# The order of the engines' queues, worked out by another of the tile layer's planners

## The chip, the cores and the metric

The kernel runs on one core of a Trainium2 chip. The metric is the device time of one execution in microseconds. Five engines work side by side, each through a queue of its own, strictly in order: TensorE (PE, matmuls and transposes), VectorE (DVE), ScalarE (ACT), GpSimd (POOL) and SyncE (SP, which issues the weight loads). An instruction whose operand isn't there yet holds up everything behind it on its engine.

## What is computed

Two transformer blocks, one after the other, on 256 rows of 1024 features, in fp32. Cut to what matters:

```python
def first_block(x, mem, ...):                       # 4 layers
    for i in range(4):
        kind = i % 3     # 0: top-k index attention, 1: dilated attention, 2: block attention
        mix = attention[kind](x @ w_in[...])        # rotary on q, k; layer norm on the index keys
        mo  = memory_attention(qm, mem_n @ w_mem_kv[i])
        x = layer_norm(ALPHA * x + concat(mix, mo) @ w_out[i])
        g, u = split(x @ w_gate_up[i])              # swiglu, 2816 wide
        x = layer_norm(ALPHA * x + (silu(g) * u) @ w_down[i])

def second_block(x, p, ...):                        # 2 layers
    for l in range(2):
        u = rms_norm(x) @ w_in[l]                   # differential, latent and sliding-window attention
        y = sum(gate_b * ((o_b * silu(z_b)) @ w_br_b[l]) for b in (a, b, c))
        x = x + rms_norm(y @ w_out[l])              # "post-norm"
        x = x + sigmoid(x @ w_ple_gate[l]) * (p[l] @ w_ple_proj[l])
```

## The kernel before

The 256 rows are two streams of 128 rows, t = 0 and 1. Each stream is a Python generator that goes through all six layers; the loop at the end of the program (L1193 to L1206) advances them in turn, stream 1 four weight units behind stream 0, so that each weight is loaded once and used by both.

A weight unit is 256 rows of at most 512 columns (`ensure`, L316): a DMA on SP's queue into `raw` (three buffers), a cast to the high part `H` on ScalarE (L330) and the rest `L` = raw - H on VectorE (L331), seven buffers of each. Activations are split likewise into `xH` and `xL`. A product is then three matmuls for each 128 rows: H with xH (L375), L with xH (L376), H with xL (L377), the output in an `mm` bank of 128 rows by up to 512 columns.

Whatever a stream has to do besides matmuls of weights is written at the place where it is wanted, or put off by some units (`defer`, `job`, `tick`, L340 to L362). The steps that matter here:

- Transposes of activations on TensorE (L398) into a `w` bank, copied out as a split: cast L413 on ScalarE and difference L414 on VectorE (L409 and L410 with a scale, L391 and L393 without a split).
- The swiglu: tanh L893 on ScalarE, L894 and the product with the up half L896 on VectorE, then `h_T` (L885) transposes the result `nat` by L398.
- Layer norms of the first block: L451, L452, then L459 and L461 on VectorE, then transposes of `x`.
- Rotary steps on GpSimd (L217 to L220), index keys on VectorE (L792 to L796) with their transposes L802.
- Dilated attention: scores L472, L727 on VectorE, exponential L731 on ScalarE, transposes L498, product L509, normalisation L516 on VectorE.
- The post-norm of the second block: square L1155 on ScalarE and copy L1157 on VectorE of each half, sum L1160, power on GpSimd (L425, L427), scale L1165 and add L1167 on VectorE for each half, transposes L398 of `x`.

The program text does not fix the order of the queues. The tile layer takes the instructions with their dependences, puts them into one queue for each engine by a list scheduler that keeps a clock of its own, and adds the semaphore waits.

Of the kernel before, what the change touches and what calls it, by code (L numbers as in the profile page):

```python
# [65 lines left out]
def tile_two_blocks(  # L66
# [7 lines left out]
    nc = tc.nc  # L74
# [24 lines left out]
    def bcast_row(ap2d, n):  # L99
        return bass.AP(tensor=ap2d.tensor, offset=ap2d.offset, ap=[[0, P], [1, n]])  # L100

# [1 line left out]
    xt = [xp.tile([P, D], F32, tag=f"x{t}", name=f"x{t}") for t in range(2)]  # L103
    cst = cp.tile([P, C_DIL], F32, name="cst")
    posi = cp.tile([P, 2, 2], I32, name="posi")
# [113 lines left out]
        eng.tensor_tensor(out=t2[:, :, half:], in0=v[:, :, :half], in1=bc(s[:, half:]), op=ALU.mult)  # L219
        eng.tensor_tensor(out=v, in0=t1, in1=t2, op=ALU.add)  # L220

# [1 line left out]
    units = []  # L223

    seq = [0]
# [156 lines left out]
        yield from gemm_part(t, acc, ck.units, xh, xl, True, True)  # L382
        return acc

# [1 line left out]
    evac_n = [0]  # L386

    def evac(dst, src, scale=None):
# [127 lines left out]
        vec.tensor_tensor(out=dst, in0=o.rearrange("p (h w) -> p h w", w=w),  # L516
                          in1=r[:, :n].unsqueeze(2).to_broadcast([P, n, w]), op=ALU.mult)

# [1 line left out]
    memT = [xp.tile([P, 4, 2 * P], F32R, tag=f"m{k}", name=f"memT{k}") for k in range(4)]  # L520

    mem_rows = []
# [50 lines left out]
            tick(t)  # L573
        evac(mem_kv[layer][:, which], acc)

# [1 line left out]
    bias_rep = dp.tile([12, P, 384], F32, tag="bias_rep", name="bias_rep")  # L577

    def prepare_bias():
# [75 lines left out]

        return job(t, a, b, c)

# [1 line left out]
    def block1(t):  # L659
        nkt = t + 1  # L660
        nk = nkt * P
# [244 lines left out]
                add_norm(t, half, acc, st)  # L906
            xT = finish_norm(t, st, gt, bt, i + 1 < DEPTH)

# [1 line left out]
    def block2(t):  # L910
        nkt = t + 1
        nk = nkt * P
# [343 lines left out]
```

## Time and profile before

| | us |
|---|---|
| median of 3 runs | 1982.85 (1980.98 to 1984.48) |
| the profiled execution, its own time | 1982.1 |
| span of the profiled execution | 1982.1 |
| TensorE busy in it | 1940.6 |
| VectorE, ScalarE, GpSimd busy | 1240.0, 981.2, 211.0 |

A row of the page or of a view names the engine, the line of the program, the operation and its tiles (out<-in, with the numbers of buffers left out). Idle time in front of an instruction is in square brackets, with the engine and line whose result ended it. A matmul's listed duration reaches from its start to its modelled end; since matmuls overlap, the pace is read from one start to the next.

### The profile page before, as it was taken

To read this page: it belongs to the slowest core of one execution; us is meant where nothing else is said; L and a number is where in the kernel's file an instruction comes from. 1 tells how busy PE (TensorE), PEld (TensorE's weight loads), DVE (VectorE), ACT (ScalarE), POOL (GpSimd) and SP (SyncE) were. 2 spreads that over 40 slices of the span, in tenths; PEclk is the share of its full clock that TensorE was granted. 3 is DMA by queue.
4 is the path that set the end of the run, shared out by engine and by line. 5 is a ranking of instruction groups with operands and counts; after the bars stand their busy time and mean duration, and the time that the engine had idled before them with its cause. 6 is when DMAs were issued, how large, how long until landed. Compare 5 with 4: busy or idle time off the path is not lost. (4 is left out here: it accounts for less than half of the span.)

```text
span 1982.1 us, 27405 instructions
## 1 busy us (share of the span) xinstructions
PE 1940.6 (98%) x10013; PEld 1612.5 (81%) x10013; DVE 1240.0 (63%) x2148; ACT 981.2 (50%) x1650; POOL 211.0 (11%) x358
## 2 busy tenths in 40 slices
PE   7999999999999999999999999999999999999998
PEld 6888778888888878888877878887888887888886
DVE  5857555657665565765567576556666667566565
ACT  5654444444444455444445544445654456665453
POOL 4020000011000012000020200002121111111010
PEclk9999999999999999999999999999999999999999
DMA  6635666544665653565654356566446655445653
GB/s 197 187 99 158 209 184 199 182 136 131 209 182 174 198 169 107 158 192 155 211 178 134 105 161 191 159 208 175 119 145 179 186 177 168 120 141 149 188 184 106
DMA packets 198295, 327.55 MB, mean 165 GB/s; under 512 B 12914, under 2 KB 70838, under 8 KB 198160
## 3 DMA queue, kind: packets, MB, share of 16 engines
q1 hardware_dynamic: 191072, 306.03, 51.1%
q0 software_dynamic: 5312, 17.44, 2.8%
q10 hardware_dynamic: 1776, 2.33, 0.3%
q8 instruction: 79, 1.29, 0.3%
q14 instruction: 56, 0.46, 0.1%
HBM read 324.68 MB, written 3.43 MB: 166 GB/s over the span
## 5 line engine op out<-in xcount | busy, mean ns | idle before, releaser
L331 DVE TENSOR_TENSOR L<-raw,H 128x1024 fp32r<-128x1024 f32 (+3 forms) x616 | 727.7, 1182 | 452.3 <-ACT H L330 447.5
L330 ACT CAST H<-raw 128x1024 fp32r<-128x1024 f32 (+3 forms) x616 | 615.5, 1000 | 593.6 <-PE mm L377 457.8
L375 PE MATMUL mm<-H,xH 128*128 128x512 f32 (+3 forms) x1904 | 741.9, 391 | 1.9 <-ACT H L330 1.7
L377 PE MATMUL mm<-H,xL 128*128 128x512 f32 (+3 forms) x1904 | 717.7, 378 | 2.1 <-DVE xL L406 1.7
L376 PE MATMUL mm<-L,xH 128*128 128x512 f32 (+3 forms) x1904 | 716.0, 377 | 0.0
L375 PEld LDWEIGHTS mm<-H,xH 128*128 128x128 f32 x1904 | 358.6, 188 | 73.3 <-issue 5.0
L377 PEld LDWEIGHTS mm<-H,xL 128*128 128x128 f32 x1904 | 358.2, 188 | 71.3 <-DVE xL L406 3.1
L376 PEld LDWEIGHTS mm<-L,xH 128*128 128x128 f32 x1904 | 359.4, 189 | 55.9 <-DVE L L331 0.5
L375 PE MATMUL mm<-H,hH 128*128 128x512 f32 x352 | 137.6, 391 | 0.0
L376 PE MATMUL mm<-L,hH 128*128 128x512 f32 x352 | 137.2, 390 | 0.0
L377 PE MATMUL mm<-H,hL 128*128 128x512 f32 x352 | 137.0, 389 | 0.0
L423 POOL TENSOR_SCALAR pw_in<-mv 128x1 f32<-128x1 f32 x22 | 15.1, 690 | 822.1 <-DVE mv L432 822.0
L489 ACT ACTIVATE sm<-sm,mn 128x128 f32<-128x128 f32 (+1 forms) x136 | 60.9, 449 | 42.2 <-DVE mn L485 41.9
L398 PE MATMUL w<-cst,nat 128*128 128x128 f32 (+1 forms) x436 | 69.9, 276 | 11.3 <-DVE nat L896 6.2
L377 PEld LDWEIGHTS mm<-H,hL 128*128 128x128 f32 x352 | 66.1, 188 | 13.7
L375 PEld LDWEIGHTS mm<-H,hH 128*128 128x128 f32 x352 | 66.1, 188 | 13.1
L376 PEld LDWEIGHTS mm<-L,hH 128*128 128x128 f32 x352 | 66.1, 188 | 13.1
L398 PEld LDWEIGHTS w<-cst,nat 128*128 128x128 f32 (+1 forms) x436 | 51.8, 139 | 29.4 <-DVE nat L896 9.6
L413 ACT CAST xH<-w 128x512 fp32r<-128x512 f32 (+1 forms) x64 | 33.4, 532 | 53.9 <-PE w L398 51.9
L217 POOL TENSOR_TENSOR rope<-nat,rc 128x128 f32<-128x128 f32 (+1 forms) x38 | 20.2, 532 | 326.8 <-ACT nat L624 286.5
L498 PE MATMUL w<-cst,sm 128*128 128x128 f32 x304 | 52.5, 276 | 0.4
L398 PE MATMUL w<-cst,x 128*128 128x128 f32 x192 | 31.3, 290 | 15.4 <-DVE x L461 5.3
(262 smaller groups left out, 2023.4 us busy)
## 6 DMA issues: line engine op xcount, KB each, us to landing
raw<-in_w_gate_up_dram SPq DMA_DIRECT2D x160, 512.0 KB, 3.7
raw<-in_w_in_dram SPq DMA_DIRECT2D x104, 512.0 KB, 3.6
raw<-in_w_down_dram SPq DMA_DIRECT2D x88, 512.0 KB, 4.4
raw<-in_w_out_dram SPq DMA_DIRECT2D x48, 512.0 KB, 3.5
raw<-in_w_in_a_dram SPq DMA_DIRECT2D x56, 256.0 KB, 3.0
raw<-in_w_in_a_dram SPq DMA_DIRECT2D x16, 512.0 KB, 5.1
raw<-in_w_mem_kv_dram SPq DMA_DIRECT2D x16, 512.0 KB, 4.1
raw<-in_w_gate_up_dram SPq DMA_DIRECT2D x32, 256.0 KB, 2.8
```

Source lines behind the costliest of these rows:

```text
L217: eng.tensor_tensor(out=t1, in0=v, in1=bc(c), op=ALU.mult)
L330: act.copy(h, raw)
L331: vec.tensor_tensor(out=lo, in0=raw, in1=h.bitcast(F32), op=ALU.subtract)
L375: pe.matmul(a, xh[:, kt, :], h[:, j, :], start=st, stop=False)
L376: pe.matmul(a, xh[:, kt, :], lo[:, j, :], start=False, stop=False)
L377: pe.matmul(a, xl[:, kt, :], h[:, j, :], start=False, stop=en)
L398: pe.transpose(tr[:width, j, :], src(j), ident)
L413: act.copy(h, tr[:, :n, :])
L423: pool.tensor_scalar(v[:, :n], src, eps, None, op0=ALU.add)
L489: act.activation(sm[:, j, :], src, AF.Exp, bias=mn[:, j : j + 1], scale=-1.0, accum_out=sums[:, j : j + 1])
L498: pe.transpose(tr[:, j * nkt + kt, :], sm[:, j, kt * P : (kt + 1) * P], ident)
```

## The change

One argument is added where the tile layer is opened; the scheduler then keeps its clock with its timeline simulator. The other lines of the diff only drop comments. Instructions, buffers and data stay; SP's queue keeps its order word for word.

```diff
-    with tile.TileContext(nc) as tc:
+    with tile.TileContext(nc, schedule_with_timeline_sim=True) as tc:
         tile_two_blocks(tc, *args)
```

Three places show what moves. In the rows, numbers behind a name tell buffers apart.

TensorE, swiglu of layer 0 of the first block; `mm_2507` is a product of stream 0, `mm_2475` one of stream 1, `nat_2395` the swiglu's result of stream 0 that the transposes L398 read. The order before:

```order
L375 MATMUL mm_2507<-H_2510,xH0_1777 128x512
L376 MATMUL mm_2507<-L_2511,xH0_1777 128x512
L377 MATMUL mm_2507<-H_2510,xL0_1778 128x512
L398 MATMUL w_2526<-cst_83,nat_2395 128x128 x4
L375 MATMUL mm_2475<-H_2426,xH1_1952 128x512
```

And now:

```order
L375 MATMUL mm_2475<-H_2426,xH1_1952 128x512
L376 MATMUL mm_2475<-L_2427,xH1_1952 128x512
L377 MATMUL mm_2475<-H_2426,xL1_1953 128x512
L375 MATMUL mm_2475<-H_2444,xH1_1952 128x512
L376 MATMUL mm_2475<-L_2445,xH1_1952 128x512
L377 MATMUL mm_2475<-H_2444,xL1_1953 128x512
L375 MATMUL mm_2507<-H_2535,xH0_1777 128x512
L375 MATMUL mm_2475<-H_2444,xH1_1952 128x512
L398 MATMUL w_2526<-cst_83,nat_2395 128x128 x4
```

The transposes have moved behind eleven matmuls: a unit and a half of stream 1 and the first matmul of stream 0's next unit, which before came after them.

TensorE, end of the dilated layer; `sm_4372` is the last head's exponentials of stream 0, `PT_4434` their transposes, `b2_0_3467` the attention's output of stream 0, `xH0_4270` its split. The order before:

```order
L498 MATMUL w_4432<-cst_83,sm_4372 128x128
L377 MATMUL mm_4419<-H_4320,xL1_4408 128x512
L472 MATMUL w_4486<-b1_0_3466,b1_1_3565 128x128
L509 MATMUL w_4436<-b1_0_3466,PT_4434 128x192
L398 MATMUL w_4441<-cst_83,b2_0_3467 128x128 x2
L472 MATMUL w_4486<-b1_1_3565 128x128
```

And now:

```order
L498 MATMUL w_4432<-cst_83,sm_4372 128x128
L509 MATMUL w_4436<-b1_0_3466,PT_4434 128x192
L398 MATMUL w_4441<-cst_83,b2_0_3467 128x128 x4
L375 MATMUL mm_4282<-H_4450,xH0_4270 128x512
L376 MATMUL mm_4282<-L_4451,xH0_4270 128x512
```

Four steps that feed each other by way of other engines (L498, L509, L398, L375) now stand in direct succession; the scores L472 and the matmul of stream 1 that stood between them come earlier.

VectorE, post-norm of the first of the second block's two layers; `x0_81` is the stream's `x`, `nat_14476` and `nat_14556` are its two halves, `nat_14652` is of stream 1. The order before:

```order
L1157 COPY nat_14556<-mm_14478 128x512
L1160 TENSOR_TENSOR tot_14558<-ssq_14371 128x1
L331 TENSOR_TENSOR L_14642<-raw_14639,H_14641 128x1024
L1165 SCALAR_TENSOR_TENSOR nat_14476<-nat_14476,pw_out_14562,gg_14369 128x512
L1165 SCALAR_TENSOR_TENSOR nat_14556<-nat_14556,pw_out_14562,gg_14369 128x512
L1167 TENSOR_TENSOR x0_81<-x0_81,nat_14476 128x512
L1167 TENSOR_TENSOR x0_81<-x0_81,nat_14556 128x512
L331 TENSOR_TENSOR L_14695<-raw_14692,H_14694 128x1024
```

And now:

```order
L1157 COPY nat_14556<-mm_14478 128x512
L1160 TENSOR_TENSOR tot_14558<-ssq_14371 128x1
L331 TENSOR_TENSOR L_14695<-raw_14692,H_14694 128x1024
L331 TENSOR_TENSOR L_14713<-raw_14710,H_14712 128x1024
L1165 SCALAR_TENSOR_TENSOR nat_14476<-nat_14476,pw_out_14562,gg_14369 128x512
L1165 SCALAR_TENSOR_TENSOR nat_14556<-nat_14556,pw_out_14562,gg_14369 128x512
L1157 COPY nat_14652<-mm_14548 128x512
L1160 TENSOR_TENSOR tot_14654<-ssq_14467 128x1
L1167 TENSOR_TENSOR x0_81<-x0_81,nat_14476 128x512
L331 TENSOR_TENSOR L_14731<-raw_14728,H_14730 128x1024
L1167 TENSOR_TENSOR x0_81<-x0_81,nat_14556 128x512
```

Two splits and the other stream's copy and sum have moved ahead of the adds L1167, and a third split stands between them. On TensorE the transposes of `x` stand 15 matmuls behind the last matmul of the product that L1157 copies, before 24.

## Rows read from the trace of the kernel before

**Rows 1.** The page, part 1: busy time, share of the span, instructions.

```profile
PE 1940.6 (98%) x10013; PEld 1612.5 (81%) x10013; DVE 1240.0 (63%) x2148; ACT 981.2 (50%) x1650; POOL 211.0 (11%) x358
```

**Rows 2.** Timeline of TensorE and VectorE at a swiglu: start, duration, instruction, [idle].

```profile
240.77 0.66 PE L398 MATMUL w<-cst,nat 128*128 128x128 f32 x4 [1.83 <-DVE nat L896]
...
241.50 0.39 PE L376 MATMUL mm<-L,xH 128*128 128x512 f32 x1
241.73 0.40 PE L377 MATMUL mm<-H,xL 128*128 128x512 f32 x1
...
238.65 1.22 DVE L331 TENSOR_TENSOR L<-raw,H 128x1024 fp32r<-128x1024 f32 x1
...
240.04 0.68 DVE L896 TENSOR_TENSOR nat<-nat,mm 128x512 f32<-128x512 f32 x1
```

**Rows 3.** Waits of TensorE: line, what for, us in total, times, longest.

```profile
PE w L398 <- DVE nat L896: 6.2, 6, 1.8
PE w L398 <- DVE x L461: 5.3, 9, 1.5
PE w L398 <- DMA cst<-in_const_dram: 4.0, 1, 4.0
PE w L398 <- POOL nat L220: 3.7, 9, 0.7
PE w L398 <- DMA x<-in_x_dram: 3.5, 1, 3.5
PE w L802 <- DVE ki L796: 2.8, 3, 1.3
PE w L398 <- DVE x L1167: 2.4, 4, 0.8
PE mm L377 <- DVE xL L406: 1.7, 2, 0.9
PE mm L375 <- ACT H L330: 1.7, 1, 1.7
PE mm L377 <- DVE pT L414: 1.4, 2, 0.7
PE w L802 <- DVE mv L432: 0.8, 1, 0.8
```

**Rows 4.** The page, part 5: groups by line; busy, mean ns, idle before, releaser.

```profile
L330 ACT CAST H<-raw 128x1024 fp32r<-128x1024 f32 (+3 forms) x616 | 615.5, 1000 | 593.6 <-PE mm L377 457.8
```

**Rows 5.** Timeline of TensorE, shortly after the first loads.

```profile
12.41 0.63 PE L377 MATMUL mm<-H,xL 128*128 128x512 f32 x1
12.84 0.63 PE L375 MATMUL mm<-H,xH 128*128 128x512 f32 x1
```

**Rows 6.** Timeline of VectorE and TensorE at the first post-norm.

```profile
1634.28 0.68 DVE L1157 COPY nat<-mm 128x512 f32<-128x512 f32 x1
...
1636.92 1.42 DVE L1165 SCALAR_TENSOR_TENSOR nat<-nat,pw_out,gg 128x512 f32<-128x512 f32 x2 [0.47 <-POOL pw_out L427]
1638.25 1.29 DVE L1167 TENSOR_TENSOR x<-x,nat 128x512 f32<-128x512 f32 x2
...
1637.80 0.39 PE L377 MATMUL mm<-H,xL 128*128 128x512 f32 x1
1639.00 1.26 PE L398 MATMUL w<-cst,x 128*128 128x128 f32 x8 [0.81 <-DVE x L1167]
```

**Rows 7.** Timeline of TensorE and ScalarE at the end of the dilated layer.

```profile
471.45 0.27 PE L498 MATMUL w<-cst,sm 128*128 128x128 f32 x1
...
474.90 0.72 PE L375 MATMUL mm<-H,xH 128*128 128x512 f32 x2
...
477.00 0.94 ACT L731 ACTIVATE sm<-sm,mn 128x768 f32<-128x768 f32 x1 [2.27 <-DVE mn L727]
```

**Rows 8.** Timeline of ScalarE, start of the feed-forward part, layer 0.

```profile
173.55 1.05 ACT L330 CAST H<-raw 128x1024 fp32r<-128x1024 f32 x1 [1.41 <-issue]
174.50 0.59 ACT L391 ACTIVATE mkv<-mm 128x512 f32<-128x512 f32 x1
```

## The prediction

> **What bounds the kernel now.** I read the page first: TensorE is busy 1940.6 us, 98% of a span of 1982.1, VectorE 63%, ScalarE 50% [rows 1]. A busy matmul is not a matmul at its peak, so the next view is TensorE's own rows: 512-column matmuls start 0.227 us apart all through the kernel, although each is listed at 0.39 us (the starts 241.50 and 241.73 in [rows 2]). At that pace the engine is full. What an order of the queues can give or take is therefore only TensorE's idle time: 1982.1 - 1940.6 = 41.5 us. The view of TensorE's waits says where it lies [rows 3]: 4.0 + 3.5 us are the first loads, which no order of these instructions shortens; after the last matmul some 5 us pass; about 27 us are short waits between 30 and 1960 us. The longest of these is 1.83 us. A wait of w us costs about w + 0.16, because a matmul that finds TensorE empty loses the overlap of 0.39 - 0.227.
>
> Who is late in these waits is nearly always VectorE (L896, L461, L1167, L796): a short step there stands behind weight splits L331 of 1.22 us, or the ScalarE step ahead of it behind casts L330 of 1.05 us. The 616 casts fill 616 us [rows 4], and as many splits somewhat more; TensorE needs their results in turn, but not each of them soon.
>
> **What the change does to the queues.** Every instruction stays, and the weight loads on SP's queue keep their order, so matmul time and bytes stay, and I cost them at nothing. What moves is the order on TensorE, VectorE and ScalarE: by some 16 places each on TensorE and VectorE. So the sum is a list of waits that go and waits that come, place by place.
>
> **Waits that go.** I take the TensorE work that stands between the matmul that starts a chain and the transposes or matmuls that need its end, in the old and in the new order, at 0.227 us a matmul.
> (a) Swiglu, L398 after L896. Before, 12 matmuls (2.7 us) stand between the end of the up product and the transposes; VectorE starts L896 at 240.04, because a split started at 238.65 is ahead of it, and TensorE stands still 1.83 us [rows 2]. After, 23 matmuls (5.2 us) stand there, against at most 4.5 us from matmul to the end of L896 in the six cases. All six waits go: 6.2 us.
> (b) Norm of the first block (L461): distance 4.9 to 6.2 us becomes 9.4 to 9.6 at five of nine waits; 2.6 of the 5.3 us go; the rest has the same distance or gets worse (below).
> (c) Rotary step on GpSimd (L220): seven of nine waits, 3.25 of 3.7 us. (d) Index keys (L796 and L432): distances 3.7 to 8.2 become 8.4 to 12.2; 2.8 + 0.8 us. (e) Entry of the second block and the branches (L406, L414 and four small ones): distance 2.7 becomes 7.5; 4.4 us. (f) The one wait for a cast, near the start: nine more matmuls (2.0 us) stand ahead of it; 1.65 us.
> Sum [rows 3]: 6.2 + 2.6 + 3.25 + 3.6 + 4.4 + 1.65 = 21.7 us in 32 waits; with 32 x 0.16 it is 26.8 us.
>
> **Waits that come.** The trace cannot show these; each is built from durations and bounded by the same chain in the old order.
> (g) Post-norm of the second block, twice (1639 and 1952 us). The chain is copy L1157, the power L427 on GpSimd, scale L1165, add L1167, transposes [rows 6]. Before, the last matmul ahead starts at 1637.80, so the transposes could start at 1638.03 and start at 1639.00: 0.97 late. After, nine matmuls fewer stand ahead: 0.97 + 9 x 0.227 = 3.0 late with the old VectorE order. That order is worse too: two splits instead of one stand ahead of L1165, the second waiting for a cast whose buffer comes free only 1.4 us of TensorE work ahead of the transposes; then L1165 twice (1.33 from start to start), L1157 with the small L1160 (0.7), L1167 (0.65, half of the two): with the cast's 1.05 that is 1.05 + 1.22 - 1.4 + 2.7 = 3.6 late, some 3.8 with the hand-overs. Third, a split now stands between the two adds: the second four transposes wait 1.22 + 0.65 - 0.4 = 1.5 more at the first place, and 0.6 at the second, where four matmuls stand between. 5.3 and 4.4 take the place, at each, of 0.97 and a wait of 0.4 on the other stream: 9.7 - 2.7 = +7.0 us. Ends: twice 3.0 - 0.97 = +4, and +9.
> (h) End of the dilated layer, stream 0 (about 474 us): four steps that feed each other now stand back to back on TensorE (L498, L509, L398, L375). Before, 471.45 to 474.90 pass between the first and the last of them without a wait [rows 7]; of that time the new order fills only 0.9 us, so some 2.5 us are lost; with a split and two L727 ahead of L516, and the exponential L731 (0.94) ahead of L413, 3.8. Two smaller ones of the kind at 444 and 465 us: 1.3. Together 5.1; ends 2.5 and 7.
> (i) Start of the feed-forward part in layers 0 and 2: on ScalarE a third cast and the copy L391 are put ahead of both L413, which stood ahead of them [rows 8]: 1.05 + 0.59 = 1.6 each, 3.2.
> (j) Attention of the two index layers at 776 and 1111 to 1120 us: 2.5. (k) Norms at 1157 and 1358 us: 1.4 + 2.7. (l) Three small ones: 1.4.
> Sum: 7.0 + 5.1 + 3.2 + 2.5 + 4.1 + 1.4 = 23.3 us. All of these come from places where steps that feed each other were pushed together; none is measured, so the range takes them at half and at more.
>
> The net is 23.3 - 26.8 = -3.5 us against the profiled execution's 1982.1: 1978.6; the median of the runs is 0.75 above that execution, so about **1979 us**.
>
> A count speaks for a small gain. Of 1,112 results that TensorE takes from the other engines, I set the work ahead of the reader against the shortest chain: less than 2 us to spare have 268 before and 144 after; nothing to spare have 16 before and 34 after. The order widens the middle and sharpens the tail.
>
> **Rivals.** A run of this kernel can tell 0.2%, about 4 us, from no change.
> 1. *The new waits are small, 1968 us.* Each lets VectorE and ScalarE catch up, so the next place is early, and a wait that comes twice in my list is paid once. With (g) to (l) at half, 12: 1982.85 - 26.8 + 12 = 1968. For it: 268 to 144, and casts idle 458 us for want of free buffers [rows 4], so these engines have time. Against it: the back-to-back rows of (g) and (h) can't be shortened by a rested engine below 4 + 2.5 us.
> 2. *Slower: the split ahead of the result that TensorE stands waiting for, 1990 us.* In (g) the new order puts splits, some for weights needed far later, ahead of a result that nothing covers. If that holds at half of the 18 results that are newly without room, 9 x 1.22 = 11 us are added: 1990; at all of them, less the five that the sum has already, 1995. It decides for slower from some six of them on (6 x 1.22 = 7.3 over 1979 is 4 over the old time). For it: the cause of the old waits is just this, in [rows 2]. Against it: VectorE is idle 37% of the span, and a split often waits for its cast while the short step runs.
> [...]
> 4. *The order does not change.* Excluded: on TensorE 7,501 rows of the two listings differ.
>
> **How the numbers follow.** Forecast as summed, 1974 to 1984: 0.40, of which 0.18 lies under 1978.9 (faster by over 0.2%) and 0.22 within. Rival 1: 0.26, faster. Rival 2: 0.20, slower. Rival 3: 0.10, slower. Nothing that can be measured for other reasons: 0.04. So faster 0.18 + 0.26 = 0.44, same 0.22 + 0.04 = 0.26, slower 0.20 + 0.10 = 0.30. Cases of both signs hold much of this; the forecast's own range is 1974 to 1984. The range goes from rival 1 with a little more, 1967, to rival 2 with a little more, 1992; it leaves out some 0.06 below and 0.09 above.
>
> **What would show it.** In TensorE's waits after: no rows for L896 and L796, at most 0.5 us for L220, under 3 us for L461 apart from 1157 and 1358; a new entry for L1167 of 8 to 10 us in four to six waits, with one of over 3 us; waits for L516, L413 and L391 near 474 us. Matmul time within 3 us of 1940.6 by the pace, else my costing of the moved matmuls at nothing is wrong. If the swiglu waits stay, the distance in the order is not what sets them, and (a) to (f) fall. If L1167 shows under 2.4 us, (g) falls and rival 1 is right. [...]

## The result: slower by 1.7%, a third of it idle time on TensorE and two thirds longer matmuls

| | before | after |
|---|---|---|
| median, us | 1982.49 | 2017.64 (2015.37 to 2021.11, four runs) |
| ratio, 95% interval | | 1.0172 [1.0157, 1.0188] |
| span of the profiled execution | 1982.1 | 2015.7 |
| TensorE busy | 1940.6 | 1963.1 |
| TensorE idle | 41.5 | 52.6 |
| mean granted clock of TensorE | 1.000 | 0.983 |

The forecast was 1979, with 1992 as the upper end. The change cost 35 us. In the profiled executions the 33.6 us are 11.1 us more idle time and 22.5 us more busy time on TensorE, for the same instructions. First the page of the kernel after, parts 1 and 2 (busy time, and the granted clock in 40 slices), which answer to [rows 1]:

```profile
PE 1963.1 (97%) x10013; PEld 1638.9 (81%) x10013; DVE 1237.0 (61%) x2148; ACT 977.6 (48%) x1650; POOL 212.9 (11%) x358
...
PEclk9979999999999999999999999999999999999999
```

The third slice (101 to 151 us) has a 7. Before, every slice has a 9. Next TensorE's waits of the kernel after (engine and line that waits, the one waited for, us in total, times, the longest), which answer to [rows 3]:

```profile
PE w L398 <- DVE x L461: 11.2, 5, 3.7
PE w L398 <- DVE x L1167: 11.0, 3, 5.3
PE mm L375 <- ACT H L330: 5.1, 2, 4.1
PE mm L375 <- ACT xH L413: 5.0, 7, 1.5
...
PE w L398 <- DVE b L516: 2.3, 3, 1.5
...
PE w L398 <- POOL nat L220: 0.5, 1, 0.5
```

The swiglu's L896 and the index keys' L796 have no row any more, and the rotary step L220 kept 0.5 us: these waits went as forecast. Two groups grew. L1167 was forecast. L461 was not: 11.2 us in five waits against 5.3 us in nine.

**Where L461 is late.** Three of the five are at the ends of layers 0 to 2, at 385, 714 and 1044 us: 3.69, 3.50 and 2.58 us. VectorE at the first of them, in the kernel before (start, us, engine, line, operation, count, idle time ahead):

```profile
373.40 0.68 DVE L451 SCALAR_TENSOR_TENSOR x<-x,mm 128x512 f32<-128x512 f32 x1
...
374.99 1.23 DVE L331 TENSOR_TENSOR L<-raw,H 128x1024 fp32r<-128x1024 f32 x1
376.13 1.41 DVE L459 SCALAR_TENSOR_TENSOR x<-x,mv,gg 128x512 f32<-128x512 f32 x2
377.45 1.41 DVE L461 SCALAR_TENSOR_TENSOR x<-x,pw_out,gb 128x512 f32<-128x512 f32 x2
```

And after, with TensorE's row that waits:

```profile
377.21 0.68 DVE L451 SCALAR_TENSOR_TENSOR x<-x,mm 128x512 f32<-128x512 f32 x1
...
378.79 1.22 DVE L331 TENSOR_TENSOR L<-raw,H 128x1024 fp32r<-128x1024 f32 x1 [0.17 <-ACT H L330]
...
380.15 1.23 DVE L331 TENSOR_TENSOR L<-raw,H 128x1024 fp32r<-128x1024 f32 x1
381.29 1.41 DVE L459 SCALAR_TENSOR_TENSOR x<-x,mv,gg 128x512 f32<-128x512 f32 x2
382.80 1.23 DVE L331 TENSOR_TENSOR L<-raw,H 128x1024 fp32r<-128x1024 f32 x1
383.95 0.68 DVE L451 SCALAR_TENSOR_TENSOR x<-x,mm 128x512 f32<-128x512 f32 x1
384.55 1.41 DVE L461 SCALAR_TENSOR_TENSOR x<-x,pw_out,gb 128x512 f32<-128x512 f32 x2
...
385.44 1.94 PE L398 MATMUL w<-cst,x 128*128 128x128 f32 x8 [3.69 <-DVE x L461]
387.20 0.79 PE L375 MATMUL mm<-H,xH 128*128 128x512 f32 x1
387.79 0.63 PE L376 MATMUL mm<-L,xH 128*128 128x512 f32 x1
388.22 0.48 PE L375 MATMUL mm<-H,xH 128*128 128x512 f32 x1
388.54 0.40 PE L376 MATMUL mm<-L,xH 128*128 128x512 f32 x1
```

From L451 to L461 pass 4.05 us before and 7.34 us after: two more splits, and the other stream's L451. TensorE's last matmul ahead starts 4.15 us behind L451 in both (377.55 and 381.36), so the difference turns into a wait. Behind it the matmuls start 0.59 and 0.43 us apart, and only from 388.5 on 0.23.

**The clock.** The granted clock in windows around that wait and around the first post-norm (window, its length, busy time and count of each engine, the granted clock of TensorE, DMA share, GB/s), kernel after:

```profile
384.80:388.20 3.40, 2.76 (x10) 2.40 (x11) 3.40 (x6) 1.78 (x3) 0.00 (x0) 0.53 0.49 150
388.20:392.00 3.80, 3.80 (x18) 3.12 (x17) 3.31 (x7) 0.00 (x0) 2.30 (x3) 0.97 0.36 102
...
1668.00:1675.00 7.00, 4.36 (x13) 3.12 (x14) 6.27 (x12) 1.62 (x3) 3.48 (x3) 0.53 0.52 165
```

The clock's records in the two profiled executions hold two values, 1.00 and 0.50. At 0.50, called half rate here, 512-column matmuls behind the first post-norm start 0.43 us apart (1673.09, 1673.52, 1673.95); ahead of it, at 1.00, 0.23 us (1664.07, 1664.30, 1664.52). The kernel after is at 0.50 in nine stretches between its first matmuls and its last few microseconds: from 122.2 us for 23.9 us; for 3.4 us each at 385.0, 716.1, 1043.8 and 1187.1; and for 6.8 us each at 490.8, 801.4, 1668.4 and 1982.4. Together that is 65 us at half rate, so at most 32 us lost, and less where TensorE idled in them; 22.5 us were measured as busy time. The kernel before has no such stretch in its profiled execution; its other executions record mean clocks from 1.000 (in one of 1978.56 us) down to 0.997 (in one of 1986.76 us), so some of them have a few.

Eight of the nine lie at or just behind waits, of 0.7 us to 5.3 us. The longest stretch doesn't. Windows over it, restricted to L375, the first matmul of each weight product (window, length, busy time and count on TensorE and of its weight loads, granted clock, DMA share, GB/s), before:

```profile
120.00:125.00 5.00, 0.95 (x2) 0.38 (x2) 1.00 0.26 96
125.00:130.00 5.00, 1.50 (x4) 0.75 (x4) 1.00 0.30 105
130.00:135.00 5.00, 1.45 (x4) 0.68 (x4) 1.00 0.06 8
135.00:140.00 5.00, 1.28 (x3) 0.44 (x3) 1.00 0.41 120
```

and after:

```profile
120.00:125.00 5.00, 0.00 (x0) 0.00 (x0) 0.72 0.63 211
125.00:130.00 5.00, 0.00 (x0) 0.00 (x0) 0.50 0.00 0
130.00:135.00 5.00, 0.00 (x0) 0.00 (x0) 0.50 0.00 0
135.00:140.00 5.00, 0.00 (x0) 0.00 (x0) 0.50 0.00 0
```

The new planner put all weight matmuls out of this stretch, so that from 117.05 to 144.91 us TensorE's queue holds nothing but the attention's small matmuls (L472, L498, L509, L398, 64 to 256 columns each). TensorE counts as busy all that time (by ends that are modelled), and its only wait there of over 0.1 us is 0.55 us, 0.4 us ahead of the fall. Before, two to four weight products stand in every 5 us among the same small matmuls.

### The profile page after: what moved, and what is told of

The parts are those of the page before. It is cut to its first block, busy times and chain, and to the rows that moved or that the text cites. A ratio compares the mean times of both kernels' runs of the same rounds, so it can differ in the third digit from the quotient of the medians.

```text
span 2015.7 us, 27443 instructions
## 1 busy us (share of the span) xinstructions
PE 1963.1 (97%) x10013; PEld 1638.9 (81%) x10013; DVE 1237.0 (61%) x2148; ACT 977.6 (48%) x1650; POOL 212.9 (11%) x358
## 4 chain that ended last, share of the span: by engine, by line
PE 92%; DVE 3%; DMA 2%; ACT 2%; issue 1%; POOL 1%; ACTq 0%; DVEq 0%; POOLq 0%
PE mm L375 25%; PE mm L377 25%; PE mm L376 25%; PE w L472 5%; PE w L398 4%; PE w L509 3%; PE mm L571 2%; PE w L498 2%; DVE L L331 1%; ACT H L330 1%; DMA raw<-in_w_gate_up_dram 1%; DMA raw<-in_w_ple_gate_dram 0%; DMA posi<-in_positions_dram 0%; DVE x L459 0%; DMA raw<-in_w_in_b_dram 0%
## 5 line engine op out<-in xcount | busy, mean ns | idle before, releaser
L375 PE MATMUL mm<-H,xH 128*128 128x512 f32 (+3 forms) x1904 | 728.7, 385 | 10.5 <-ACT H L330 5.1
L376 PE MATMUL mm<-L,xH 128*128 128x512 f32 (+4 forms) x1904 | 725.8, 382 | 1.3 <-DVE L L331 1.2
L375 PEld LDWEIGHTS mm<-H,xH 128*128 128x128 f32 x1904 | 361.1, 190 | 79.3 <-ACT xH L413 8.8
L375 PE MATMUL mm<-H,hH 128*128 128x512 f32 x352 | 137.2, 390 | 0.0
L375 PEld LDWEIGHTS mm<-H,hH 128*128 128x128 f32 x352 | 66.2, 188 | 13.3
L413 ACT CAST xH<-w 128x512 fp32r<-128x512 f32 (+1 forms) x64 | 32.5, 532 | 86.7 <-PE w L398 86.6
L398 PE MATMUL w<-cst,nat 128*128 128x128 f32 (+1 forms) x436 | 69.3, 275 | 0.5 <-POOL nat L220 0.5
L398 PEld LDWEIGHTS w<-cst,nat 128*128 128x128 f32 (+1 forms) x436 | 54.1, 142 | 11.2 <-POOL nat L220 0.8
L498 PE MATMUL w<-cst,sm 128*128 128x128 f32 x304 | 60.5, 290 | 0.6 <-DVE mn L485 0.5
L414 DVE TENSOR_TENSOR xL<-w,xH 128x512 fp32r<-128x512 f32 (+1 forms) x64 | 38.3, 618 | 36.8 <-ACT xH L413 36.4
L398 PE MATMUL w<-cst,x 128*128 128x128 f32 x192 | 33.5, 318 | 27.0 <-DVE x L461 11.2
```

Source lines behind the costliest of these rows:

```text
L375: pe.matmul(a, xh[:, kt, :], h[:, j, :], start=st, stop=False)
L376: pe.matmul(a, xh[:, kt, :], lo[:, j, :], start=False, stop=False)
L398: pe.transpose(tr[:width, j, :], src(j), ident)
L414: vec.tensor_tensor(out=lo, in0=tr[:, :n, :], in1=h.bitcast(F32), op=ALU.subtract)
L498: pe.transpose(tr[:, j * nkt + kt, :], sm[:, j, kt * P : (kt + 1) * P], ident)
```

## The experiments

**Theory W** (waits): the new waits at the norms, post-norms and the dilated layer make the kernel slower, with the clock's fall behind each as a part of its price. **Theory C** (clock): at 122 us it is the kind of work that stands together on TensorE, with no wait at all, and that alone costs some 10 us. **Rival**: the loss is spread over the whole order and belongs to no place.

All kernels are the kernel before with the same addition, a table that fixes each engine's queue, as an order of issue and without waits. Only the table differs, unless said otherwise: with VectorE alone edited, for instance, TensorE's and ScalarE's rows stand in the trace in the very order of the kernel that was edited.

```diff
         tile_two_blocks(tc, *args)
+        pin(tc, nc)
+
+def pin(tc, nc):
...
+            if prev is not None:
+                tc.add_manual_dep(have[name], prev, info, reason="order")
+            prev = name
```

**One step of VectorE alone, at five norms.** From the kernel after, the split goes behind L461 (and behind L1167 at the post-norms). VectorE's order there:

```diff
 L451 SCALAR_TENSOR_TENSOR x_81<-x_81,mm 128x512
 L452 BN_STATS st<-x_81 128x6
-L331 TENSOR_TENSOR L<-raw,H 128x1024
 L432 BN_AGGR mv<-st 128x2
 L331 TENSOR_TENSOR L<-raw,H 128x1024
 L459 SCALAR_TENSOR_TENSOR x_81<-x_81,mv,gg 128x512 x2
-L331 TENSOR_TENSOR L<-raw,H 128x1024
+L461 SCALAR_TENSOR_TENSOR x_81<-x_81,pw_out,gb 128x512 x2
+L331 TENSOR_TENSOR L<-raw,H 128x1024 x2
 L451 SCALAR_TENSOR_TENSOR x_82<-x_82,mm 128x512
-L461 SCALAR_TENSOR_TENSOR x_81<-x_81,pw_out,gb 128x512 x2
```

> The kernel after, its queues written out as they are, with VectorE alone edited at five places (the norms of x at 380, 709 and 1039 us of its trace, the post-norms at 1664 and 1977): the splits L331 that stand among L452, L432, L459, L461 or among L1160, L1165, L1167 are put behind the last of these, all but one. Theory 'waits and clock': TensorE's waits for L461 fall from 11.2 to about 3 us, those for L1167 from 11.0 to some 6, and the half-rate stretches that follow these places (3.4 or 6.8 us each, 24 us in all) go too; 12 to 18 us of idle time and 8 to 12 us of half rate, so about 1990 to 1997 against 2017.6. Rival 'waits alone' (half rate costs nothing, since TensorE would have waited for the other engines anyway): 2000 to 2006. Rival 'splits that are later starve the matmuls': new waits for L331, at or above 2010.

Measured: 2014.70 us, ratio 1.0158 [1.0141, 1.0175]; some 3 us back instead of 20 or more, which the intervals don't tell from none. TensorE at the end of layer 0 in this kernel, and ScalarE ahead of it:

```profile
380.82 1.29 PE L398 MATMUL w<-cst,x 128*128 128x128 f32 x8 [0.70 <-DVE x L461]
384.60 0.67 PE L375 MATMUL mm<-H,xH 128*128 128x512 f32 x1 [2.50 <-ACT xH L413]
...
383.02 1.04 ACT L330 CAST H<-raw 128x1024 fp32r<-128x1024 f32 x1 [1.59 <-DMA raw<-in_w_in_b_dram]
383.97 1.07 ACT L413 CAST xH<-w 128x512 fp32r<-128x512 f32 x2
```

The wait for L461 fell from 3.69 to 0.70 us as meant, but the next one took its place: the transposes are done, and ScalarE has a weight cast queued ahead of L413, and that cast starts only at 383.02, when its weights have landed. The half-rate stretches stayed at four of the five places, 27.3 us there against 23.9; the one at the third layer end went. So it is not VectorE's splits alone: the new planner moved the casts and TensorE's own rows with them.

**The reverse, in the kernel before.** One split of VectorE is moved ahead of L459 (or L1165) at the same five places.

```diff
-L331 TENSOR_TENSOR L<-raw,H 128x1024
+L331 TENSOR_TENSOR L<-raw,H 128x1024 x2
 L459 SCALAR_TENSOR_TENSOR x_81<-x_81,mv,gg 128x512 x2
```

> The kernel before, its queues written out, with VectorE alone edited at the same five norms: the one split L331 that comes next in its queue is moved ahead of L459 (or L1165). Five splits change their place, nothing else. By the rows of before the wait of TensorE at each grows from 0.4 or 0.8 to about 4 us: +17 us of idle time in all. Theory 'waits and clock': after each of them TensorE runs at half rate for a stretch of 3.4 us or more, and the time is 1982.5 + 17 + 6 to 12 = 2005 to 2011, mean clock about 0.99. Rival 'waits alone': 1999, clock 1.00. Rival 'made up later': under 1992.

Measured: 1987.59 us, ratio 1.0025 [1.0015, 1.0034]. Waits grew to 1.16 to 1.85 us only, because the split's cast came earlier than assumed. The granted clock fell for 3.4 us in three places, of which only one (695.7 us) is among the five; the other two (19.9 and 241.7 us) stand where nothing was moved, behind waits of 1.81 and 2.36 us that the kernel before has with 1.65 and 1.83. A single split does not explain the loss.

**Which half of the program.** The kernel before's order up to 165 us and the order after from there on; and the other way round.

> The order of before up to the point where layer 0's attention ends (165 us of its trace), the order of after for all that is left. Matching instructions of the two traces, after is 7.6 us later than before at that point. Theory 'bunch' (27 us in which TensorE's queue holds only the attention's small matmuls run at half rate): no half-rate stretch before 370 us, and 2017.6 - 7.6 = 2010, give or take 2 for the border. Rival 'made up later': 2017.

Measured: 2009.92 us, ratio 1.0132 [1.0117, 1.0147], and no half-rate stretch before 377 us.

> The other half: the order of after up to the end of layer 0's attention (172.5 us of its trace), the order of before for the rest. TensorE waits less in that stretch in after (6.0 us of idle time between 5 and 165 us against some 8 in before), so the rival 'waits alone' gives 1982.5 - 2 = 1980. Theory 'bunch and clock': half rate from about 122 to 146 us as in after, and 1982.5 + 7.6 = 1990, mean clock about 0.994.

Measured: 1988.90 us, ratio 1.0026 [1.0015, 1.0037]. Its only half-rate stretch between start and end is at 123.1 us, for 20.5 us. Its page, part 1, against [rows 1]:

```profile
PE 1949.4 (98%) x10013; PEld 1623.0 (82%) x10013; DVE 1239.1 (62%) x2148; ACT 981.4 (49%) x1650; POOL 214.1 (11%) x358
```

TensorE is busy 8.8 us longer than in the kernel before and idle 2.9 us less (38.6 of 1988.0 against 41.5). Theory C's place alone makes the kernel slower, although it waits less, and before the first layer end of the new order is reached. Net it costs 5.7 us here, and 7.7 by the other half. The larger part of the loss lies behind it.

**The first stretch without its cause.** The last kernel (the order after up to the end of layer 0's attention), with 18 more matmuls of constants, 256 columns each, among the attention's own between 118 and 140 us. They are unused work: the bank that they write is overwritten by the real product.

```diff
+    def fill(bank):
+        fills[0] += 1
+        if fills[0] in FILL:
+            pe.matmul(bank[:, 0:256], ident, causal, start=True, stop=True)
```

> bpfx (after's order to the end of layer 0's attention, before's for the rest) with 18 more matmuls of 256 columns on constants, put between the attention's small matmuls of the 25 us at 118 to 143 us; each writes a bank that the next real matmul overwrites. By the scores of 256 columns they cost 0.24 us each at full rate: 4.3 us more work. Theory 'the clock falls because that stretch streams too little': with the columns the clock stays up for all or most of it, 25 us become 14 + 4, and the time is 1989 - 7 = 1982, with more work. Rival 'the clock falls for another reason': half rate as before, 1989 + 9 = 1998. Rival 'half rate costs little, the chain sets the pace': 1989 to 1993.

Measured: 1988.13 us, ratio 1.0028 [1.0018, 1.0038], no slower than without the added work. By its time alone that lies next to the third expectation, half rate costs little; what decides is the rows. The windows of the kernel without the matmuls, and with them:

```profile
125.00:130.00 5.00, 5.00 (x24) 4.67 (x24) 1.68 (x5) 0.93 (x4) 0.00 (x0) 0.50 0.00 0
130.00:135.00 5.00, 5.00 (x24) 4.45 (x23) 1.73 (x8) 1.48 (x5) 0.00 (x0) 0.50 0.00 0
```

```profile
125.00:130.00 5.00, 5.00 (x32) 4.11 (x33) 2.01 (x9) 2.44 (x10) 0.00 (x0) 1.00 0.00 0
130.00:135.00 5.00, 5.00 (x36) 4.27 (x35) 2.31 (x9) 1.09 (x4) 0.00 (x0) 1.00 0.01 3
```

With them TensorE stays at 1.00 through the whole attention (one stretch of 3.4 us comes later, at 245.3 us, at a swiglu wait of 2.35 us). The stretch without weight matmuls takes 26.2 us at half rate (115.82 to 142.02) and 24.75 us (116.84 to 141.59) with the added work, of which that work fills 7.9 us (18 x 0.44, its own pace) to 9.2 us (from each start to the next row's). So the same attention took 15.6 to 16.9 us at 1.00. Of the 26.2 us, 18.9 lie behind the fall of the clock, and by my estimate half the clock can have cost them at most half, 9.5 us; so its price is about 9.4 us (26.2 - 16.9), near the 8.8 us of busy time above. I had expected the added work to cost 0.24 us each, 4.3 in all; each of these f32 matmuls appears as two instructions in its row and takes 0.44 us, about twice that, which ate the gain. Shown is that the work on TensorE there decides whether the clock falls at 122 us, with no idle time to speak of. The added matmuls also close the wait of 0.55 us, but longer ones pass without a fall elsewhere (1.50 us at 1157 us in the kernel before). Not shown is what about the attention's matmuls does it: their columns, their kind (many are transposes), or gaps between them that modelled ends hide.

**The norms and post-norms.** The kernel after, with the order of the kernel before on all engines around the three layer ends and the first post-norm, and from just ahead of the second post-norm to the end.

```diff
 L451 SCALAR_TENSOR_TENSOR x_82<-x_82,mm 128x512
-L461 SCALAR_TENSOR_TENSOR x_81<-x_81,pw_out,gb 128x512 x2
-L331 TENSOR_TENSOR L<-raw,H 128x1024
+L414 TENSOR_TENSOR xL_3447<-w,xH_3446 128x512 x2
 L452 BN_STATS st<-x_82 128x6
-L414 TENSOR_TENSOR xL_3447<-w,xH_3446 128x512 x2
+L331 TENSOR_TENSOR L<-raw,H 128x1024
```

> The order of after, with the order of before put in on all engines around the same five norms (364 to 398, 690 to 728, 1008 to 1045, 1625 to 1661 us and from 1936 us of the trace of before), so that ScalarE's casts there are put back too and not only VectorE's splits. In a_norm5, where only VectorE was edited, the wait for L461 went and one of 2.5 to 2.8 us for the copies L413 and L414 behind it came, with the same half-rate stretch. Theory: both queues hold the place; with both put back the five waits and their half-rate stretches go, and by the lateness of matching instructions of after over before, which grows by 4.8, 2.7, 0.7, 5.2 and 5 us there, the time is 2017.6 - 18 = 1999. Rival 'the wait moves on again': 2012 or more.

Measured: 1992.18 us, ratio 1.0049 [1.0031, 1.0066]: 25.5 us below the kernel after, more than expected. The waits at these places shrink:

```profile
PE w L398 <- DVE x L461: 2.9, 5, 1.2
PE w L398 <- DVE x L1167: 2.5, 3, 1.2
```

L461 and L1167 cost 22.2 us of waiting in the kernel after and 5.4 here, 16.8 less; other waits grew by some 3, and in the profiled executions (1994.4 against 2015.7, this one the slowest of its four) idle time is 13.7 us less and busy time 7.6. Of the stretches at half rate, those at the three layer ends and at the second post-norm are gone, and 3.4 us of 6.8 are left at the first; in all 37.5 us at half rate are left of 65, which is where the busy time went.

**The dilated layer.** The kernel after, with the order before from 400 to 541 us.

> The order of after, with that of before between 400 and 541 us of the trace of before (the dilated layer's attention, out product and the norm behind it). Matching instructions: after loses 10.1 us there. Theory: the steps that feed each other back to back cost it, with the half-rate stretch of 6.8 us at 490: 2017.6 - 10 = 2007.5. Rival 'made up later': 2015 or more.

Measured: 2006.02 us, ratio 1.0115 [1.0098, 1.0131]; 11.6 us back, as expected. The stretch that was put back holds 5.5 us of idle time in the kernel after (3.7 at the places that I had priced at 5.1, the rest at 509 to 535 us) and 0.2 here, and its half-rate stretch is gone.

**Waits of a chosen size.** The kernel before in its own order, with 2, 4 or 6 more norm statistics, unused, on VectorE ahead of the first L461 or L1167 at the five places.

```diff
+            for _ in range(SLOW_N):
+                vec.bn_stats(small(6, "junk"), src)
```

> The kernel before, its queues written out, with two extra VectorE reads of x (bn_stats, results unused, some 0.63 us each) put right ahead of the first L461 or L1167 at the same five norms; no other row moves. The wait of TensorE at each grows by 1.3 us, to 1.7 or 2.1. Waits alone: 1982.5 + 5 x 1.3 = 1989, clock 1.00. If waits of this length already let the clock fall for a stretch of 3.4 us (1.7 us lost at each): up to 1997.

> The same with four reads at each place: waits of 2.9 or 3.3 us. Waits alone: 1982.5 + 5 x 2.5 = 1995, clock 1.00. Waits and clock: a half-rate stretch of 3.4 to 6.8 us follows all or most of them, 1.7 to 3.4 us lost at each: 2003 to 2012, clock 0.991 to 0.996.

> The same with six reads: waits of 4.2 or 4.6 us, as long as the longest of after. Waits alone: 1982.5 + 5 x 3.8 = 2001.5. Waits and clock: 2010 to 2018, of which 8 to 17 are the half rate.

| added to each | wait at the five places, us | median, us | ratio | by waits alone | more than that |
|---|---|---|---|---|---|
| 2 | 1.78 to 2.00 | 1992.44 | 1.0044 [1.0029, 1.0059] | 1989 | +3.4 |
| 4 | 2.97 to 3.18 | 2002.46 | 1.0088 [1.0067, 1.0108] | 1995 | +7.5 |
| 6 | 4.15 to 4.37 | 2009.44 | 1.0129 [1.0113, 1.0145] | 2001.5 | +7.9 |

Each wait costs more than its length, by some 1.5 us on average where the wait is 3 us or more; TensorE's rows, matched with those of the kernel before, give 0.6 to 2.5 us at the single places. The first kernel shows what the extra is. Its clock fell behind the first two of the five waits only: there TensorE lost 3.0 and 2.9 us for 1.4 us more of waiting. At the other three, where the clock stayed, it lost 1.2 to 1.4 us, the wait alone. One place of the third, in windows up to the wait, around its end (380.91) and later:

```profile
372.00:380.00 8.00, 4.76 (x21) 3.59 (x20) 7.85 (x13) 3.16 (x3) 2.05 (x2) 1.00 0.51 158
380.00:387.00 7.00, 6.09 (x18) 5.03 (x19) 6.20 (x9) 2.11 (x3) 0.87 (x1) 0.52 0.00 0
387.00:394.00 7.00, 7.00 (x37) 5.77 (x37) 5.54 (x9) 1.84 (x4) 1.78 (x3) 0.99 0.85 265
```

18 matmuls in the 7 us from the last of the wait of 4.15 us on, 37 in the next 7. The price of a wait is its length and the half-rate stretch behind it; theory W needs both.

**The good parts alone.** The order of the kernel before for attentions, norms and post-norms, that of after for feed-forward parts and for the second layer block's projections and branches.

> The order of before for the attentions, the norms and the post-norms, that of after for the feed-forward parts (190 to 362, 541 to 691, 859 to 1008, 1199 to 1331 us of the trace of before) and for the second block's projections, attention and branches (1367 to 1607, 1661 to 1918): the stretches in which matching instructions say that after gains 4.3, 1.3, 0.5, 0.5, 2.9 and 4.9 us. If the gains are real and stand alone: 1982.5 - 14 = 1968, clock 1.00. If they are owed to the losses ahead of them (a TensorE that came late finds the others ahead): 1978 to 1983.

Measured: 1968.75 us, ratio 0.9930 [0.9915, 0.9945], faster than either kernel, mean clock 1.000 in the profiled execution; against the kernel before, idle time is 9.7 us less and busy time 5.5. The rows for the waits, and the page's first line:

```profile
PE w L398 <- DVE x L461: 6.1, 9, 1.5
PE w L802 <- DVE ki L796: 3.3, 3, 1.8
PE w L398 <- DVE x L1167: 2.4, 4, 0.8
...
PE 1935.1 (98%) x10013; PEld 1614.9 (82%) x10013; DVE 1238.5 (63%) x2148; ACT 981.1 (50%) x1650; POOL 213.0 (11%) x358
```

So part of the forecast's gain is real, 13.6 us of 26.8, and the places with the loss can be cut away from it. The three groups found account for it: 2017.6 less 25.5 (norms), 11.6 (dilated layer) and 7.7 (the first attention: the kernel with the order before up to 165 us, against after) is 1972.8, near that.

Last, the same with other cuts, and splits put behind L796:

> best1 with two changes: the change-over from after's order to before's ahead of the norms at 691 and 1008 us moved to 680 and 1000, where best1 kept a wait of 1.20 us instead of 0.40; and on VectorE the splits L331 that stand between L792 and L796 (index keys) put behind L796, where TensorE waits 1.79 and 1.26 us in the second index layer. If the split ahead is what holds these: 1.5 to 3 us less than best1, 1966 to 1967. Rival (the chain itself is that long, or the splits are then late): 1968 to 1970.

Measured: 1969.32 us, ratio 0.9929 [0.9914, 0.9944]. The wait for L796 fell from 3.3 to 1.8 us, but the first load's cast waits 2.2 us instead of 1.0: no change.

## Why the prediction was wrong, step by step

- **What bounds it.** Right that TensorE bounds the kernel. Wrong in "What an order of the queues can give or take is therefore only TensorE's idle time": the order also gave 22.5 us of busy time, since it decides which matmuls stand together (about 9 us of it at 122 us). That sentence is the step at which the prediction failed first, and with it "matmul time and bytes stay, and I cost them at nothing": the term priced at nothing is two thirds of the loss.
- **Waits that go.** (a), (c) and (d) held: no L896, no L796, 0.5 us left of L220. (e) left 1.4 us at L406. (f) is gone at its place, but a wait of 4.10 us for a cast came among the first loads, where one of 3.45 shrank to 0.86. The gain shows in the mixed kernel, which has the new order at (a) and at the second block's entries and branches, and keeps 3.3 us for L796 and 2.0 for L220.
- **(b), the layer ends, failed.** It took the TensorE work ahead of the transposes for the measure and left a place with "the same distance" as it was. VectorE's own order there has two more splits, and ScalarE's a cast ahead of L413. At these three places the waits are 9.8 us in all, where (b) left 2.7 for everything it didn't remove. Rival 2 named this cause, splits ahead of the result, but at other places; and taking the splits away by themselves gave back only 3 us. By the prediction's sums idle time should have come to 41.5 - 21.7 + 23.3 = 43.1 us; it came to 52.6, and the layer ends (9.8 us, 1.2 before) are nearly all of the difference.
- **(g), the post-norms, held in sum, not in its parts.** Forecast 3.8 + 1.5 and 3.8 + 0.6 us, measured 5.10 + 0.62 and 5.25 with no second wait for L1167. Rows of VectorE and TensorE in the kernel after show the step that was named, against [rows 6]: both splits start behind TensorE's last matmul (1664.52), 2.5 us, where the sum counted one, partly covered.

```profile
1664.85 2.51 DVE L331 TENSOR_TENSOR L<-raw,H 128x1024 fp32r<-128x1024 f32 x2 [0.97 <-ACT H L330]
1667.28 1.41 DVE L1165 SCALAR_TENSOR_TENSOR nat<-nat,pw_out,gg 128x512 f32<-128x512 f32 x2
...
1670.01 1.11 PE L398 MATMUL w<-cst,x 128*128 128x128 f32 x4 [5.10 <-DVE x L1167]
```

- **(h), the dilated layer, held in its place**, with 0.37, 0.67 and 1.49 us at 486 to 490 us and 1.1 us at 463 to 476, 3.7 in all where 5.1 was forecast. Its price did not: 11.6 us came back when it and 1.8 us of waits behind it were undone, the 6.8 us at half rate among them.

```profile
486.82 0.59 PE L509 MATMUL w<-b,PT 128*128 128x192 f32 x2 [0.37 <-ACT PT L391]
...
488.30 0.44 PE L398 MATMUL w<-cst,b 128*128 128x128 f32 x2 [0.67 <-DVE b L516]
490.23 0.50 PE L375 MATMUL mm<-H,xH 128*128 128x512 f32 x1 [1.49 <-ACT xH L413]
```

- **(i) and (k) came smaller:** 0.94 us twice where (i) had 1.6; at (k)'s two norms, forecast 1.4 and 2.7, the transposes start without a wait (1188.0 and 1388.6 us).
- **Rival 3, a lower clock behind the new waits, was right in kind and had 0.10.** Matmuls 0.43 us apart stand in [rows 5], behind waits of 3.99 and 3.45 us; whether the clock was lower there no run shows, since the trace's records of it begin at 14.8 us. What the runs show is the same pace behind (g), 0.43 us, with the clock recorded at 0.50. Stretches at 0.50 follow (g) twice and (h); at (k) one lies at the first norm, behind another wait (1.52 us for L516), and none at the second. The chosen waits put the price of one at some 1.5 us. Not among these places are the three layer ends (3.4 us at 0.50 each), which (b) had passed over, and above all the stretch at 122 us (23.9 us), where hardly a wait stands. Nothing in the prediction looked for it, though the new order shows it, with no weight matmul between 117 and 145 us. At the first layer end the clock fell to 0.50 behind a wait of 3.69 us; at 122 us it fell with a wait of 0.55 us.
- **The test was the right one.** "Matmul time within 3 us of 1940.6" was to show whether moved matmuls cost nothing. It came to 1963.1, and they don't.
- **The count of results with room** (268 down to 144 with under 2 us) was read as a sign for a small gain. It counts places, and the loss lay in a few.

What stays open: two stretches at half rate, at 801 and 1187 us, 6.8 and 3.4 us, were not undone by themselves, so their share is not measured. They stand in the kernel with the dilated layer put back. They are gone in the kernel with the old order around the norms, with VectorE alone edited there, and with the old order up to 165 us, though all these keep the order after at both places and the same waits ahead of them (0.71 and 1.52 us). So these two are not owed to the order of those places alone; what decides, no run here shows.

## What to carry to other kernels

Where an order of instructions changes, read it for what now stands together on the bounding engine, as well as for who waits: in one place, where heavy matmuls had stood spread among small ones, pulling them ahead brought the granted clock down to 0.50, which cost about 9 us, 6 to 8 net of the waits it saved. At each place where the order changes, follow the whole chain through every engine's queue, and price a wait of TensorE at its length plus the half-rate stretch that may follow it (some 1.6 us where 3.4 us followed here). A planner's order can be taken in parts: its good places and its bad ones add up almost separately.

## What was unexpected of the hardware

- TensorE's granted clock read 0.50 for 23.9 us, with a longest wait of 0.55 us just ahead of it and a busy share of 100% in the windows; 18 added matmuls of 256 columns among them kept it at 1.00.
- After waits of almost one size the clock sometimes fell and sometimes not: it stayed after 1.83 us in the kernel before [rows 2] and after one of 3.0 us for L896 in the kernel with the new order up to the end of layer 0's attention, and fell for 3.4 us after waits of 1.8 to 2.4 us elsewhere. With two statistics added it fell behind two waits of 1.78 us and not behind a third. A price of a wait is thus a mean over such cases.
- Each of the 18 added f32 matmuls of 256 columns appears as two instructions and takes 0.44 us at its own pace (0.51 to the next row).
